# Moving SBUF tiles by 32, 64 or 96 bytes: spacers between the pools of a two-block transformer kernel

## The chip, the cores and the metric

The kernel runs on one core of one Trainium2 chip. The metric is the device time of one execution in microseconds (us), the median of several runs. TensorE is the engine PE of the profile (its weight loads are the row PEld), VectorE is DVE, ScalarE is ACT, GpSimd is POOL and SyncE is SP.

## The reference, cut to what matters

512 tokens of 1024 features pass two blocks. The first has two layers: a gated linear recurrence (HGRN2) and a differential attention, each followed by a squared-ReLU MLP of 4096 features. The second block has a state space branch and a windowed attention that are gated and summed, then a cross attention to 256 memory rows, then a third MLP of the same shape. All arithmetic is float32. Nearly all the work is products of activations with weights:

```python
def squared_relu_mlp(h, w_up, w_down):
    u = jax.nn.relu(h @ w_up)
    return (u * u) @ w_down
...
        proj = h @ w_in[i]
...
        merged = (jax.nn.sigmoid(gate_a) * (attn @ w_attn_branch[i])
                  + jax.nn.sigmoid(gate_b) * (ssd @ w_ssd_branch[i]))
        x = x + merged @ w_out[i]
        h = rmsnorm(x, norm_cross[i])
        x = x + cross_attention(h, rmsnorm(mem, norm_mem[i]), w_xq[i], w_xkv[i], w_xo[i])
        h = rmsnorm(x, norm_ffn[i])
        x = x + jnp.square(jax.nn.relu(h @ w_up[i])) @ w_down[i]
```

## The kernel before, in words

Every float32 product with weights is made of three products of the rounded type float32r. Each operand is held as a high part and a low part, and `mm3` (lines 397 to 400) sums high by high (L398), high by low (L399) and low by high (L400) into one PSUM tile:

```python
    def mm3(ps, a, b, first, last):
        nc.tensor.matmul(ps, a[0], b[0], start=first, stop=False)
        nc.tensor.matmul(ps, a[0], b[1], start=False, stop=False)
        nc.tensor.matmul(ps, a[1], b[0], start=False, stop=last)
```

The operand `a` is the stationary one: 128 columns of it are loaded into the array before each product. The operand `b` is the moving one: its 256 or 512 columns stream through the array. The profile names a product `out<-moving,stationary`.

The weights come from DRAM into the pool `raw` (three tiles of 4096 bytes per partition, names `raw`), and `Weights._split` (L115 to L127) splits each into a tile `hl` of the pool `spl` (six tiles of 8192 bytes: a high half and a low half). ScalarE writes the high part (L119, L125), VectorE, and in eight units GpSimd, the low part (L121, L126). The units are used in one fixed order. Loads run three tiles ahead and splits six tiles ahead of the first unit in use.

The activations lie in fixed tiles. `XTh` and `XTl` (pool `fix`) hold the transposed block input, `UAh` and `UAl` (pool `fix`) the first four tiles of 128 features of an intermediate result, and `UBh` and `UBl` (pool `bp`, opened much later) the other four. `h` and `ACC` (pool `fix`) hold the residual stream and a sum. The work tile `WK` (in the state space branch `WS`) and the evacuation tiles `y` hold what stays in float32, and `WR` the split keys of the attentions. `ident` (pool `const`) is the identity that every transpose streams.

Two kinds of loop call `mm3`:

- `feat` and `feat_first` put features on the partitions. They load 128 columns of `hl` as the stationary operand and stream the activations: 512 columns in `feat`, 256 in `feat_first` and for the memory rows (these lie in the `UB` tiles).
- `tok`, `tok2` and `last_rows` put tokens on the partitions. They load 128 tokens of `XT`, `UA` or `UB` as the stationary operand and stream `hl`: 256 columns in `tok`, 512 in `tok2` and `last_rows`.

The two calls, first of `feat`, then of `tok2`:

```python
                mm3(ps[:, :width], (wh[:, c], wl[:, c]), src(k), k == 0, k == n_k - 1)
...
                mm3(ps, (xh[:, tk], xl[:, tk]), w[k], k == 0, k == n_k - 1)
```

The order on each engine comes from a scheduler; the order of the weights from the list of units; the rest from waits on tiles.

The pools lie in SBUF one behind the other in the order in which they are opened: `const`, `fix`, `raw`, `spl`, `sm`, and then what the phases open (`bp`, `ev`, `wp` or `sp`). A tile begins at the next multiple of 32 bytes, so the lengths of the pools ahead of it set where it begins. All large tiles are multiples of 128 bytes long, so all tiles of one pool have the same remainder by 128.

Of the kernel before, what the change touches and what calls it, by code (L numbers as in the profile page):

```python
# [18 lines left out]
P = 128  # L19
# [7 lines left out]
def shape_constants():  # L27
    """Arrays that depend on shapes alone."""
    s = np.arange(P)[:, None]
    t = np.arange(P)[None, :]  # L30
    ident = np.eye(P, dtype=np.float32)
    lev = []
    for b in (1, 2, 4, 8, 16, 32, 64):
        same = (s // (2 * b)) == (t // (2 * b))
        lev.append(same & ((s // b) % 2 == 0) & ((t // b) % 2 == 1))
    lev.append(s <= t)
    masks = np.stack(lev, 1).astype(np.float32)
    d = np.arange(640) - 511
    n = np.abs(d)
    first = [8, 12, 16, 23, 32, 46, 64, 91]  # L40
    large = 8 + sum((n >= f).astype(np.int64) for f in first[1:])
    bucket = np.where(d > 0, 16, 0) + np.where(n < 8, n, large)
    onehot = -(bucket[None, :] == np.arange(32)[:, None]).astype(np.float32)
    rel = P + s - np.arange(3 * P)[None, :]
    band = np.where(np.abs(rel) <= 128, np.abs(rel), BIG).astype(np.float32)
    sel = np.zeros((P, 2, P), np.float32)
    sel[P - 1, 0, :] = 1.0
    sel[0, 1, :] = 1.0
    return {
        "c_ident": ident,  # L50
        "c_masks": np.ascontiguousarray(masks),
        "c_onehot": onehot,
        "c_band": band,
        "c_sel": sel,
    }


def vw(ap, off, dims):
    """A view of an SBUF/PSUM access pattern with its own free dimensions."""
    return bass.AP(tensor=ap.tensor, offset=ap.offset + off, ap=[list(ap.ap[0])] + [list(x) for x in dims])  # L60
# [6 lines left out]
class Weights:  # L67
    """Weight units in the order of their use: loaded ahead, split into two float32r parts ahead."""
# [13 lines left out]
    @staticmethod  # L82
    def _parts(sp):
        """a unit comes in parts of the tiles of rows that fill a place"""
        return max(1, sp[1] // Weights._rows(sp))
# [44 lines left out]
    def ahead(s, i):  # L130
        """i: the first unit that is still to be used."""
        n = s.first[-1]
        while s.n_spl < n and s.n_spl < s.first[i] + s.live:
            s._loads()
            s._split(s.n_spl)
            s.n_spl += 1
        s._loads()
# [10 lines left out]
    def get(s, name, hold=None):  # L148
        """The next unit; hold: the unit that stays the first one in use."""
        i = s.n_get  # L150
        assert s.specs[i][0] == name, (s.specs[i][0], name)
        s.n_get += 1
        s.ahead(i if hold is None else hold)
        assert len(s.hl[i]) == s._parts(s.specs[i]), name
        r = s.hl.pop(i)
        return [(h[:, k], l[:, k]) for h, l in r for k in range(h.shape[1])]


class Work:
    """Fixed places in one tile, by phase; what follows waits by the overlap of places."""  # L160
# [23 lines left out]
def together(*works, until=None):  # L184
    """the steps of several pieces of work in turn, up to the mark (if given) or the end of each"""
    works = list(works)
    while works:
        for w in list(works):
            try:
                mark = next(w)  # L190
            except StopIteration:
                works.remove(w)
                continue
            if until and mark == until:
                works.remove(w)


def body(ctx, tc, I, out, dbg=None, stop=None):
# [18 lines left out]
    # ------------------------------------------------------------ weights  # L217
# [93 lines left out]
    # split beside the norms at the ends of phases, where VectorE has the most to do  # L311
    WT.on_pool = {"m0up00", "m0up01", "m1up00", "m1up01", "sx0", "sbc0", "m2up00", "m2up01"}

    # ------------------------------------------------------------ fixed places
    h = fix.tile([P, NT, D], F32, name="h")
    ACC = fix.tile([P, NT * D], F32, name="ACC")
    acc = ACC.rearrange("p (t d) -> p t d", t=NT)
    XTh = fix.tile([P, 8, S], F32R, name="XTh")
    XTl = fix.tile([P, 8, S], F32R, name="XTl")
    UAh = fix.tile([P, 4, S], F32R, name="UAh")  # L320
    UAl = fix.tile([P, 4, S], F32R, name="UAl")

    ident = const.tile([P, P], F32, name="ident")
# [34 lines left out]
    # ------------------------------------------------------------ second arenas  # L358
# [12 lines left out]
    def open_wk(rounded=0):  # L371
        """the work tile, and places for operands of float32r products"""
        if "wctx" in st:
            st["wctx"].close()
        st["wctx"] = ExitStack()
        wp = st["wctx"].enter_context(tc.tile_pool(name="wp", bufs=1))
        n = 8424 - rounded
        st["wk"] = Work(wp.tile([P, n], F32, name="WK"), n)
        if rounded:
            r = wp.tile([P, rounded], F32R, name="WR")  # L380
            return [r[:, i:i + 512] for i in range(0, rounded, 512)]
# [20 lines left out]
    def split(dst, src, scale=None):  # L402
        """dst: float32r pair; src: PSUM or SBUF float32; scale: None or a per-partition factor."""
        hi, lo = dst
        if scale is None:
            nc.scalar.activation(out=hi, in_=src, func=AF.Copy)  # L406
            nc.vector.tensor_tensor(out=lo, in0=src, in1=hi.bitcast(F32), op=ALU.subtract)  # L407
        else:
            nc.scalar.activation(out=hi, in_=src, func=AF.Copy, scale=scale)  # L409
            nc.vector.scalar_tensor_tensor(out=lo, in0=src, scalar=scale, in1=hi.bitcast(F32), op0=ALU.mult, op1=ALU.subtract)  # L410

    def split_q(hd, ps):
        """two maps of 64 features, scaled: for each one tile with the high part where it is and the low part in the
        other half of the partitions"""
# [16 lines left out]
    def norm_places(first, n):  # L431
        """for the norms at the end of a phase: places from the end of the work tile"""
# [11 lines left out]
    def inv_sqrt(x, width):  # L444
        """x ** -0.5 without another table of ScalarE"""
# [11 lines left out]
    def row_rstd(src, k="", fine=False):  # L457
        """1 / rms of the rows; fine: the first half of a row alone as soon as it is there"""
# [10 lines left out]
    def gains(*aps):  # L469
        """norm weights on every partition, in the last places of the work tile"""  # L470
# [7 lines left out]
    def norm_T(t, src, gain, dst, fine=False):  # L478
        """rms norm of the rows of a token tile, and its transpose into the pair dst(kb) of [P, 4, n]"""
# [19 lines left out]
    # ------------------------------------------------------------ products  # L499
    def feat(w, src, evac, n_k=8, width=S):  # L500
        """features on partitions: two column tiles of the unit"""
# [8 lines left out]
    def feat_first(ws, src, evacs):  # L510
        """the same for the first units of a phase, half of the tokens at a time"""
# [14 lines left out]
    def tok(w, src, evac, n_k=8, tiles=NT):  # L526
        """tokens on partitions; evac(t, [P, 2, 256]) for two token tiles at a time"""
# [10 lines left out]
    def tok2(w, src, evac, n_k=8):  # L538
        """the same for units of 512 columns; evac(t, [P, 512])"""
# [8 lines left out]
    def last_rows(name, src, evac, done):  # L548
        """four resident units of the last part of a sum, one token tile after the other"""
# [21 lines left out]
    def post_norm(t, fine=False):  # L571
        """h += rms_norm(acc) * GP"""
# [11 lines left out]
    # ------------------------------------------------------------ MLP  # L584
# [35 lines left out]
    # ============================================================ layer 0: HGRN2  # L620
# [35 lines left out]
    def tables():  # L656
        # small tables
# [45 lines left out]
        # minus the relative bias, by distance  # L703
# [23 lines left out]
    def hgrn_head(hd, Z, G):  # L727
# [6 lines left out]
        def scores(b=0):  # L734
            """inside each chunk; for the larger blocks the pairs of blocks alone"""
# [136 lines left out]
    # ============================================================ MLP 0, and the norms of layer 1  # L872
# [10 lines left out]
    # ============================================================ layer 1: differential attention  # L883
# [7 lines left out]
    def diff_head(hd, k, v, place):  # L891
# [12 lines left out]
        def weights(i):  # L904
            """exponentials of row tile i for both maps"""
# [50 lines left out]
    def k_evac(j):  # L956
        """the high parts on both halves of the partitions, and the low parts"""
# [86 lines left out]
    # ============================================================ block 2: the state space branch  # L1044
    close_b()
    st["ctx"] = ExitStack()
    SW = 15592
# [74 lines left out]
    def bc64(ap):  # L1122
        """[P, 4] over 64 columns each"""
# [4 lines left out]
    class Group:  # L1128
        """four heads that share B and C"""
# [21 lines left out]
        def turn(s):  # L1151
            """x and B with the tokens on partitions"""
# [27 lines left out]
        def decays(s, c):  # L1180
            """the products of C and B inside a chunk with their decays and steps"""
# [10 lines left out]
        def first(s):  # L1192
            """products of C and B, decays, states"""
# [22 lines left out]
        def second(s):  # L1216
            """the chunks' results, gated"""
# [25 lines left out]
        def third(s):  # L1243
            """norm, features on partitions"""
# [51 lines left out]
    # ============================================================ block 2: windowed attention, gates  # L1296
# [4 lines left out]
    def gk_evac(n, ps):  # L1301
        """high and low parts, each on both halves of the partitions"""
# [12 lines left out]
    class Head:  # L1315
# [7 lines left out]
        def weights(s, n):  # L1323
            """exponentials of row tile n"""
# [87 lines left out]
    # memory for the cross attention  # L1412
# [25 lines left out]
    # ============================================================ block 2: cross attention  # L1438
# [71 lines left out]
    # ============================================================ block 2: MLP, last norm  # L1510
# [44 lines left out]
```

## Time and profile before

| | |
|---|---|
| time, median of 3 runs (lowest to highest) | 2630.79 us (2628.68 to 2632.54) |
| the profiled execution: time of the core, first to last instruction | 2630.0 us |
| mean granted TensorE clock | 0.992 of full speed |
| PE busy, PEld busy | 97%, 83% of the span |
| DVE, ACT, POOL busy | 56%, 43%, 7% of the span |
| DMA, mean over the span | 93 GB/s |

The span of the profiled execution is also its time: nothing lies around it. PE is called busy from a product's start to its modelled end, and consecutive products overlap in that reading: one of 512 columns is drawn 0.39 us long while the next begins 0.23 us later. So the busy time of PE and the mean duration of a product don't tell how fast products follow each other. That is read from the starts in the timeline, or from a stretch that holds nothing but products of one form: its length over their number.

### The profile page before, as it was taken

The numbers are of one execution on the slowest core, as the hardware profiler recorded it, in microseconds if no ns is written. First come the engines' busy times: TensorE is split into PE (matmuls) and PEld (weight loads), VectorE is DVE, ScalarE is ACT, GpSimd is POOL, SyncE is SP. The second block draws the span as 40 slices with busy tenths as digits, with TensorE's granted clock in tenths as the row PEclk, the third lists the DMA queues.
The fourth block names the chain that finished last, engine by engine and source line by source line (L and its number), as shares of the span: only waits on it lengthen the run. The fifth ranks groups of instructions, "written<-read, shape, count | busy, mean of one in ns | idle before, by whom it ended". The sixth has DMA issues, their size and how long they took to land.

```text
span 2630.0 us, 36139 instructions
## 1 busy us (share of the span) xinstructions
PE 2563.8 (97%) x14312; PEld 2196.0 (83%) x14312; DVE 1483.1 (56%) x2865; ACT 1137.8 (43%) x2153; POOL 183.5 (7%) x189
## 2 busy tenths in 40 slices
PE   8999999999999989999999999999999999999999
PEld 7899888888888878888887798888888789888887
DVE  5576453344666663333477888787554466534434
ACT  6333443233475553322365545553554436423322
POOL 1100210000201030000121000000000000100000
PEclk9999999999999999999999999999999999999999
DMA  5511233233233223333324334442211233233331
GB/s 178 137 52 62 81 104 94 91 96 101 85 91 94 73 81 97 96 96 96 92 77 129 97 97 115 105 110 80 81 41 49 87 98 121 80 91 97 101 97 56
DMA packets 198904, 243.65 MB, mean 93 GB/s; under 512 B 9744, under 2 KB 153344, under 8 KB 198736
## 3 DMA queue, kind: packets, MB, share of 16 engines
q1 hardware_dynamic: 188976, 207.97, 26.0%
q0 software_dynamic: 9040, 30.76, 4.6%
q10 hardware_dynamic: 720, 2.62, 0.3%
q8 instruction: 112, 1.84, 0.3%
q14 instruction: 56, 0.46, 0.1%
HBM read 239.05 MB, written 7.51 MB: 94 GB/s over the span
## 4 chain that ended last, share of the span: by engine, by line
PE 84%; DVE 5%; issue 4%; DMA 4%; ACT 3%; POOL 0%; SPq 0%; POOLq 0%; DVEq 0%; ACTq 0%
PE psm L398 23%; PE psm L399 23%; PE psm L400 23%; DMA WS<-aD 2%; PE pss L1356 2%; PE pss L740 1%; DMA raw<-in_a_w_in_dram 1%; PE pss L1331 1%; PE pss L398 1%; PE pss L400 1%; PE pss L399 1%; PE pss L912 1%; PE pss L1352 1%; DVE WS L1118 1%; DVE hl L121 1%
## 5 line engine op out<-in xcount | busy, mean ns | idle before, releaser
L398 PE MATMUL psm<-XTh,hl 128*128 128x512 f32 (+1 forms) x1400 | 533.9, 382 | 5.7 <-ACT XTh L406 3.0
L399 PE MATMUL psm<-XTl,hl 128*128 128x512 f32 (+1 forms) x1400 | 533.8, 381 | 4.7 <-DVE XTl L407 4.7
L400 PE MATMUL psm<-XTh,hl 128*128 128x512 f32 (+1 forms) x1400 | 532.6, 381 | 0.0
L119 ACT ACTIVATE hl<-raw 128x1024 fp32r<-128x1024 f32 x321 | 338.5, 1056 | 433.6 <-PE psm L400 373.2
L121 DVE TENSOR_TENSOR hl<-raw,hl 128x1024 fp32r<-128x1024 f32 x305 | 377.2, 1237 | 248.0 <-ACT hl L119 245.1
L398 PEld LDWEIGHTS psm<-XTh,hl 128*128 128x128 f32 x1400 | 264.6, 189 | 55.5 <-ACT XTh L406 4.1
L399 PEld LDWEIGHTS psm<-XTl,hl 128*128 128x128 f32 x1400 | 264.9, 189 | 53.0 <-DVE XTl L407 5.3
L400 PEld LDWEIGHTS psm<-XTh,hl 128*128 128x128 f32 x1400 | 264.8, 189 | 48.5 <-issue 0.4
L398 PE MATMUL psm<-hl,XTh 128*128 128x256 f32 (+1 forms) x928 | 285.7, 308 | 10.2 <-DVE sk L1207 2.8
L398 PE MATMUL psm<-hl,UAh 128*128 128x512 f32 (+1 forms) x768 | 276.7, 360 | 7.7 <-DVE ACC L566 5.9
L400 PE MATMUL psm<-hl,XTl 128*128 128x256 f32 (+1 forms) x928 | 283.7, 306 | 0.0
L399 PE MATMUL psm<-hl,XTh 128*128 128x256 f32 (+1 forms) x928 | 283.2, 305 | 0.2 <-DVE hl L126 0.2
L400 PE MATMUL psm<-hl,UAl 128*128 128x512 f32 (+1 forms) x768 | 274.3, 359 | 0.2 <-DVE UAl L410 0.2
L399 PE MATMUL psm<-hl,UAh 128*128 128x512 f32 (+1 forms) x768 | 274.2, 357 | 0.0
L398 PE MATMUL psm<-hl,UBh 128*128 128x512 f32 (+1 forms) x512 | 199.8, 390 | 1.1 <-ACT UBh L409 0.8
L399 PE MATMUL psm<-hl,UBh 128*128 128x512 f32 (+1 forms) x512 | 199.0, 389 | 0.0
L400 PE MATMUL psm<-hl,UBl 128*128 128x512 f32 (+1 forms) x512 | 198.9, 389 | 0.0
L398 PEld LDWEIGHTS psm<-hl,XTh 128*128 128x128 f32 x928 | 179.8, 194 | 19.2 <-ACT hl L119 3.2
L399 PEld LDWEIGHTS psm<-hl,XTh 128*128 128x128 f32 x928 | 179.8, 194 | 7.4 <-issue 1.1
L400 PEld LDWEIGHTS psm<-hl,XTl 128*128 128x128 f32 x928 | 179.6, 194 | 6.1 <-issue 0.5
L398 PEld LDWEIGHTS psm<-hl,UAh 128*128 128x128 f32 x768 | 146.6, 191 | 31.0 <-DVE ACC L566 6.8
L400 PEld LDWEIGHTS psm<-hl,UAl 128*128 128x128 f32 x768 | 146.5, 191 | 22.0 <-issue 0.9
(402 smaller groups left out, 3862.6 us busy)
## 6 DMA issues: line engine op xcount, KB each, us to landing
raw<-in_mlp_w_up_dram SPq DMA_DIRECT2D x64, 512.0 KB, 4.3
raw<-in_mlp_w_down_dram SPq DMA_DIRECT2D x64, 512.0 KB, 3.7
raw<-in_w_in_dram SPq DMA_DIRECT2D x60, 512.0 KB, 3.8
WS<-aD POOLq DMA_DIRECT2D x32, 512.0 KB, 6.5
raw<-in_w_up_dram SPq DMA_DIRECT2D x32, 512.0 KB, 4.0
raw<-in_w_down_dram SPq DMA_DIRECT2D x32, 512.0 KB, 3.7
raw<-in_w_in_dram SPq DMA_DIRECT2D x33, 256.0 KB, 3.9
raw<-in_a_w_in_dram SPq DMA_DIRECT2D x16, 512.0 KB, 3.8
```

The lines of the kernel that those rows point to most:

```text
L119: s.nc.scalar.activation(out=h, in_=r, func=AF.Copy)
L121: eng.tensor_tensor(out=l, in0=r, in1=h.bitcast(F32), op=ALU.subtract)
L398: nc.tensor.matmul(ps, a[0], b[0], start=first, stop=False)
L399: nc.tensor.matmul(ps, a[0], b[1], start=False, stop=False)
L400: nc.tensor.matmul(ps, a[1], b[0], start=False, stop=last)
L740: nc.tensor.matmul(ps[:, tk], H[:, tk], F[:, tk], start=True, stop=True)
L912: nc.tensor.matmul(pss[m][:, :N], q[r0], kl[r0, :N], start=False, stop=True)
L1118: nc.vector.scalar_tensor_tensor(out=dst[:, o0:o1], in0=ps[:, o0 + d:o1 + d], scalar=cw(j), in1=dst[:, o0:o1], op0=ALU.mult, op1=ALU.add)
L1331: nc.tensor.matmul(ps[:, :wd], uk(s.i)[s.p][:, n * P:(n + 1) * P], k_hl[x][s.kv][:, lo * P:hi * P], start=x == 0, stop=x == 1)
L1352: nc.tensor.transpose(pt[:, j * P:(j + 1) * P], e[:, j * P:(j + 1) * P], ident)
L1356: nc.tensor.matmul(po[r0, n * P:(n + 1) * P], v[:, lo + j, s.kv * 64:(s.kv + 1) * 64], PT[:, j * P:(j + 1) * P], start=j == 0, stop=j == h ...
```

## The change

Three small tiles are added that nothing reads, and three that hold work become shorter.

- `const` begins with a spacer `pad` of 32 bytes.
- In `fix`, a gap of 64 bytes stands between `ACC` and `XTh`, and another behind `UAl`.
- The work tiles `WK` (8424 words less those of `WR`) and `WS` (15592 words) are made 40 words shorter, which makes room for the spacers.

Each spacer is written once by a memset on POOL. No loop, operand, shape or wait is changed otherwise (the other lines of the diff take out comments and docstrings).

```diff
+    def gap(pool_, name):
+        nc.gpsimd.memset(pool_.tile([P, 16], F32, name=name), 0.0)
     h = fix.tile([P, NT, D], F32, name="h")
     ACC = fix.tile([P, NT * D], F32, name="ACC")
     acc = ACC.rearrange("p (t d) -> p t d", t=NT)
+    gap(fix, "gap0")
     XTh = fix.tile([P, 8, S], F32R, name="XTh")
     XTl = fix.tile([P, 8, S], F32R, name="XTl")
     UAh = fix.tile([P, 4, S], F32R, name="UAh")
     UAl = fix.tile([P, 4, S], F32R, name="UAl")
+    gap(fix, "gap1")
+    def spacer(pool_, words):
+        pad = pool_.tile([P, words], F32, tag="pad", name="pad", bufs=1)
+        nc.gpsimd.memset(pad, 0.0)
+    spacer(const, 8)
     ident = const.tile([P, P], F32, name="ident")
...
-        n = 8424 - rounded
+        n = 8384 - rounded
...
-    SW = 15592
+    SW = 15552
```

This is where the tiles begin in a partition of SBUF, as the remainder of the address by 128 bytes:

| tiles | before | with the change |
|---|---|---|
| `ident` | 0 | 32 |
| `h`, `ACC` | 96 | 0 |
| `XTh`, `XTl`, `UAh`, `UAl` | 96 | 64 |
| `raw`, `hl` | 96 | 0 |
| `UBh`, `UBl`, `GP`, `y`, `WK`, `WS` | 32 | 64 |
| `WR` | 64 | 64 |

Slices of the large operands start at multiples of 512 bytes inside their tiles, so this remainder is also that of every operand of `mm3`.

On PE, DVE, ACT and SP the instructions stand in the same order as before. POOL's queue has the three memsets more. Its beginning (the constants, a memset of the small tile `mhalf`, and the first loads of gains and tables into `ACC` and `band`) reads before:

```order
L1551 UNCONDITIONAL_BRANCH
L325 MEMSET mhalf 128x4
L345 DMA ACC<-in_a_norm_pre_dram 8x128
L659 DMA band<-in_c_band_dram 128x384
L672 DMA ACC<-in_conv_w_dram 96x128
```

The same place with the change, the spacers' tiles being `gap_80`, `gap_86` and `pad`:

```order
L1563 UNCONDITIONAL_BRANCH
L316 MEMSET gap_80 128x16
L316 MEMSET gap_86 128x16
L332 MEMSET pad 128x8
L337 MEMSET mhalf 128x4
L357 DMA ACC<-in_a_norm_pre_dram 8x128
L671 DMA band<-in_c_band_dram 128x384
```

The three memsets stand ahead of the first DMA of POOL's queue; nothing else has moved.

## Rows read from the trace of the kernel before

**Rows 1.** Profile page: span and the busiest engine.
```profile
span 2630.0 us, 36139 instructions
...
PE 2563.8 (97%) x14312; PEld 2196.0 (83%) x14312; DVE 1483.1 (56%) x2865; ACT 1137.8 (43%) x2153; POOL 183.5 (7%) x189
```

**Rows 2.** Profile page: chain of work that ended last, by engine.
```profile
PE 84%; DVE 5%; issue 4%; DMA 4%; ACT 3%; POOL 0%; SPq 0%; POOLq 0%; DVEq 0%; ACTq 0%
```

**Rows 3.** Lines by form, PE, first line of `mm3`: count | busy us, mean ns | idle.
```profile
L398 PE MATMUL psm<-XTh,hl 128*128 128x512 f32 x1232 | 484.1, 393 | 2.6 <-DVE WS L1118 2.4 <-DVE ss L451 0.3
...
L398 PE MATMUL psm<-hl,XTh 128*128 128x256 f32 x800 | 235.1, 294 | 9.4 <-DVE sk L1207 2.8 <-ACT XTh L406 2.5 <-DVE WS L1118 2.3
...
L398 PE MATMUL psm<-hl,UAh 128*128 128x512 f32 x512 | 201.2, 393 | 1.4 <-ACT UAh L409 0.8 <-DVE ACC L566 0.3 <-DVE h L566 0.3
...
L398 PE MATMUL psm<-hl,UBh 128*128 128x512 f32 x480 | 190.3, 396 | 1.1 <-ACT UBh L409 0.8 <-DVE ACC L566 0.3
...
L398 PE MATMUL psm<-hl,UAh 128*128 128x256 f32 x256 | 75.5, 295 | 6.2 <-DVE ACC L566 5.6 <-ACT ACC L564 0.7
...
L398 PE MATMUL psm<-hl,XTh 128*128 128x512 f32 x128 | 50.6, 396 | 0.8 <-ACT WK L1388 0.8
...
L398 PE MATMUL psm<-XTh,hl 128*128 128x256 f32 x160 | 46.6, 295 | 3.0 <-ACT XTh L406 3.0
L398 PE MATMUL pss<-XTh,hl 128*128 128x256 f32 x160 | 46.2, 289 | 0.0
...
L398 PE MATMUL psm<-hl,UBh 128*128 128x256 f32 x32 | 9.5, 295 | 0.0
...
L398 PE MATMUL psm<-UBh,hl 128*128 128x256 f32 x32 | 9.0, 280 | 0.0
```

**Rows 4.** Windows of products alone: stretch, length, busy (x) by engine, PEclk, DMA.
```profile
2535.72:2579.26 43.54, 43.54 (x193) 36.05 (x192) 20.90 (x24) 16.42 (x22) 0.00 (x0) 1.00 0.38 119
2579.26:2601.02 21.76, 21.76 (x97) 18.02 (x96) 9.53 (x12) 4.19 (x5) 0.00 (x0) 1.00 0.08 25
2601.02:2623.19 22.17, 22.17 (x96) 17.86 (x95) 9.99 (x17) 5.02 (x11) 0.57 (x1) 1.00 0.18 67
1850.69:1862.20 11.51, 11.51 (x98) 11.51 (x96) 5.34 (x8) 5.56 (x8) 0.00 (x0) 1.00 0.32 91
```

**Rows 5.** Timeline of PE, first and last of two series of 256 columns.
```profile
2185.95 0.28 PE L398 MATMUL psm<-UBh,hl 128*128 128x256 f32 x1
...
2193.61 0.28 PE L400 MATMUL psm<-UBh,hl 128*128 128x256 f32 x1
...
2194.72 0.28 PE L399 MATMUL psm<-hl,UBh 128*128 128x256 f32 x1
...
2199.95 0.28 PE L400 MATMUL psm<-hl,UBl 128*128 128x256 f32 x1
```

**Rows 6.** Windows of float32 work on PE: transposes, products of 256 and of 128 columns.
```profile
1769.00:1770.20 1.20, 1.20 (x14) 1.20 (x12) 0.56 (x1) 1.18 (x4) 0.45 (x1) 1.00 0.50 176
1630.92:1632.43 1.51, 1.51 (x8) 1.33 (x7) 1.41 (x5) 0.63 (x1) 0.00 (x0) 1.00 0.33 115
...
1793.60:1794.49 0.89, 0.89 (x11) 0.89 (x9) 0.89 (x2) 0.89 (x2) 0.00 (x0) 1.00 0.02 5
```

**Rows 7.** Windows, PE instructions that read `hl` alone: state space branch, first stretch.
```profile
1315.00:1841.00 526.00, 416.73 (x2393) 0.98 0.38 101
0.00:131.50 131.50, 91.85 (x529) 0.99 0.55 158
```

**Rows 8.** Chain that ended last in these two stretches, by line.
```profile
by line: issue 18.3%; DMA WS<-aD 11.9%; PE psm L398 11.1%; PE psm L400 10.8%; PE psm L399 10.7%; DVE WS L1118 3.8%; PE pss L1238 3.3%; DVE hl L121 2.6%; ACT WS L1189 1.9%; PE pss L1169 1.6%; PE pss L1225 1.6%; PE pss L1227 1.5%; ACT hl L119
...
by line: DMA raw<-in_a_w_in_dram 22.3%; PE psm L398 17.7%; PE psm L400 17.4%; PE psm L399 17.3%; PE pss L740 5.8%; PE pss L795 3.4%; PE pss L491 2.3%; DVE hl L126 2.2%; ACT hl L125 1.7%; PE pss L744 1.5%; DVE WK L758 1.0%; PE pss L711 0.9%;
```

**Rows 9.** Timeline of POOL at the start: two memsets in a row.
```profile
0.30 0.11 POOL L1543 MEMSET const-bfloat16-1.0<- 128x1 bf16 x1
0.33 0.11 POOL L1543 MEMSET const-uint8-127<- 128x1 uint8 x1
```

## The prediction

> **What bounds the kernel now.** The first view is the page's table of engines: PE is busy for 2563.8 of 2630.0 us, DVE, the next, for 56% [rows 1]. The second is the chain of work that ended last: 84% of it is PE [rows 2]. So nearly everything that makes products follow each other faster or slower reaches the end. How fast they follow is read from stretches that hold nothing but products of one form (length over number), and there the granted clock is 1.00, that is 2.4 GHz: 512 columns are 213.3 ns, 256 are 106.7 ns.
>
> The reader is to see that these products are never that fast, and that their spacing goes with the place of the operands:
> - 512 columns of `XT` over stationary `hl`: 43.54 us for 192, 226.8 ns each. 512 columns of `hl` over stationary `UA`: 21.76 us for 96, 226.7 ns [rows 4].
> - the same product a moment later, 512 columns of `hl` over stationary `UB`: 22.17 us for 95, 233.4 ns [rows 4].
> - 256 columns of `hl` over `XT`: 11.51 us for 96, 119.9 ns [rows 4].
> - 256 columns of `hl` over `UB`: from 2194.72 to 2199.95 us 46 products, 113.7 ns. 256 columns of `UB` over `hl`: from 2185.95 to 2193.61 us 65 products, 117.8 ns [rows 5].
>
> `XT`, `UA` and `hl` all begin at remainder 96; `UB` alone begins at 32, so 64 bytes away from `hl`. Above the bare columns the five forms lose 13.4, 20.0, 13.2, 7.0 and 11.1 ns. In columns of 0.417 ns these are 32, 48, 32, 17 and 27. With four-byte columns 16 columns are 64 bytes: four of the five losses lie near a multiple of that, one to three pieces of 64 bytes. That no wait is involved is seen in the windows: PE is busy throughout. As a measure of what remains without such a loss I take the float32 work: 11 transposes of 128 columns start in 1.20 us, 109.1 ns each, and 7 passes of 256 columns in 1.51 us, 215.7 ns each [rows 6]. They go at half the pace and lose 2.4 ns above their columns.
>
> **The change, part by part.** *The operands of the products.* Before, every one begins in the middle of a piece of 64 bytes (remainders 96 and 32); afterwards none does, and the operand that is loaded lies 64 bytes from the one that streams (0 and 64). No row shows a float32r product with both operands on multiples of 64 bytes, so its spacing is bounded. Below: bare columns, 213.3 and 106.7 ns, a gain of 13.4 or more. Above: what the rows with 64 bytes between the operands show, 233.4 ns for 512 columns, a loss of 6.6, and 117.8 or 113.7 ns for 256. I take columns plus 2.4 ns, 215.7 and 109.1: the whole pieces of 64 bytes look like an extra fetch for a first half piece and collisions of two streams that walk over the same memory, and the change takes the ground from both. This is a reading of five numbers, not shown.
>
> The numbers of products are three times those of L398, since `mm3` has three of each [rows 3]:
> - 512 columns, `XT` and `UA`: 3 x (1232 + 512 + 128) = 5616, by 226.8 - 215.7 = 11.1 ns: 62.3 us.
> - 512 columns, `UB`: 3 x 480 = 1440, by 17.7 ns: 25.5 us.
> - 256 columns, `XT` and `UA`: 3 x (800 + 256 + 160 + 160) = 4128, by 119.9 - 109.1 = 10.8 ns: 44.6 us.
> - 256 columns, `UB`: 96 by 4.6 and 96 by 8.7 ns: 1.3 us.
>
> That is 133.7 us. Not all of it reaches the end. In the state space branch (1315 to 1841 us) 2393 of these products run [rows 7], at 11 ns 26.3 us; the chain there is products of `mm3` for 11.1 + 10.8 + 10.7 = 32.6%, the rest is the load of `aD`, issue, DVE and ACT [rows 8]. I keep a third and give back 17.7 us: what is late next there is the broadcast load of `aD` and the DVE work behind it. In the first 131.5 us 529 products [rows 7] would save 5.8 us; 52% of the chain is theirs, and the load of `in_a_w_in` holds 22% [rows 8]: 2.8 us go back. Sum: 133.7 - 20.5 = 113.2 us, 85% of the gross gain.
>
> *Other operands.* `ident` leaves remainder 0 for 32, while `WK`, `WS` and `y` go from 32 to 64. A transpose that streams `ident` from 0 takes 109.1 ns; a float32 product with both operands at 32 takes 0.89 us for 8, 111.3 ns [rows 6]. So some 800 transposes may lose 2.2 ns each (1.8 us) and as many or more float32 products gain it. I set the two against each other: 0, within 3 us either way. For DVE, ACT and DMA no row of this kernel ties a duration to a remainder; most of their work is beside PE's [rows 1], and I cost it at nothing. If that cover went, the splits of `hl` would be late first.
>
> *The memsets.* Two small memsets in a row on POOL start 0.03 us apart [rows 9]; three put the first load of POOL's queue back by 0.1 us, at most 0.33 us if their 0.11 us add up. Behind it waits the first split of weights. Below what is told apart here.
>
> The profiled execution took 2630.0 us, 0.8 us under the median of the runs. 2630.0 - 113.2 = 2516.8; I predict 2517 us.
>
> A rule of the Trainium skill speaks against all of this: the page "SBUF — State Buffer", section "A bandwidth-pool intuition that's wrong (but worth ruling out)", gives TensorE a second, independent read port for weight loads, and its section "SBUF: two separate sides" says that PE never waits on anyone there. By it, no placing of the operands could matter, and the sum would be 0 instead of 113 us (rival D). The trace doesn't agree: 226.7 and 233.4 ns for the same form, 44 us apart in one loop [rows 4].
>
> **The rivals.**
> - *B, half of it.* Only the half piece at the start goes, 16 columns or 6.7 ns in each of the 11280 products: 75.2 us, and 63.9 at 85%. 2566 us. For it: 256 columns of `hl` over `UB` lose 17 columns, the least of all, with nothing but the start to blame. Against: it needs a collision that is the same 64 bytes apart as at no distance.
> - *E, only products of 256 columns gain.* The 512 ones keep 226.8 ns (those of `UB` come down to it): 1440 x 6.6 = 9.5 us, with 45.9 us of the 256 ones 55.4, at 85% 47. 2583 us. For it: 64 bytes apart helped 256 columns and not 512.
> - *C, slower.* 64 bytes between the operands are what costs: 512 columns of `XT` and `UA` take the 233.4 ns of `UB`. 5616 x 6.6 = 37.1 us are lost. 256 columns gain what `UB`'s rows show: 3168 with `hl` streaming by 6.2 ns, 960 with `XT` streaming by 2.1 ns, 21.7 us. The net loss is 15.4 us: 2645 us. For it: the only rows of 512 columns with that distance. Against: in them both operands also begin in the middle of a piece. It decides from about 230.6 ns for 512 columns upward, where 5616 x 3.8 ns eat the 21.7 us.
> - *D, no change.* The remainder doesn't matter, and `UB` is slower or faster for another reason. 2630 us. Against: rows 4 and 5 differ by form and place alone.
>
> **How the numbers follow.** The forecast has a chance of 0.46, B 0.17, E 0.13, something between the forecast and B 0.04, C 0.14, D 0.06. The lowest time is that of bare columns: 2.4 ns less in 11280 products, 27 us, 23 at 85%: 2494, and with 3 us for the other operands about 2490. Up to E with its own spread the range is 2490 to 2600 us and holds 0.80. The forecast's own range is 2490 to 2545. About 0.2% (5 us) is what a measurement of this kernel can tell from no change. Faster by more: forecast, B, E and what lies between, 0.80, less 0.01 for spread: 0.79. Within it: D and the edges of the others, 0.07. Slower: C, 0.14.
>
> **What would show each step right or wrong.** In stretches of one form the profile of the changed kernel should show about 216 ns for 512 columns, alike for `XT`, `UA` and `UB`, and about 109 ns for 256. 220 and 113 would be B, 227 and 109 E, 233 C. The state space branch should shorten by less than its products do, with DVE's share up. The forecast would be wrong if 512 columns stay above 220 ns, if the two directions (activations or weights streaming) part, if the splits of `hl` no longer keep ahead of PE in the MLPs, or if the granted clock falls with denser work.

## The result, and the profile with the change

| | before | with the change |
|---|---|---|
| time, median of 4 runs each (lowest to highest) | 2631.66 us (2628.68 to 2635.60) | 2645.98 us (2645.73 to 2646.09) |
| the profiled execution, first to last instruction | 2630.0 us | 2644.0 us |

The kernel became slower: ratio 1.0059, 95% interval 1.0043 to 1.0074, some 14 us. The forecast of 2517 us and its range are missed, on the wrong side; rival C had 2645 us.

The page of the changed kernel, its span and the table of engines:

```profile
span 2644.0 us, 36142 instructions
...
PE 2579.8 (98%) x14312; PEld 2187.7 (83%) x14312; DVE 1481.9 (56%) x2865; ACT 1137.2 (43%) x2153; POOL 185.1 (7%) x192
```

Against [rows 1] PE alone has become busier by more than 2 us: 16.0 us more for the same 14312 products (the weight loads, PEld, have 8.3 us less). The three more instructions on POOL are the memsets. PE's share of the chain is 84% as in [rows 2]. So nothing points to a new wait; the products themselves follow each other more slowly. That is read where [rows 4] and [rows 5] read it, in stretches of one form. The windows of the changed kernel (stretch, length, PE busy and products, granted clock, DMA share, GB/s; the x counts also a product or two that began ahead of the window, so lengths are divided by 192, 96, 95, 96, 96 and 48):

```profile
2547.84:2592.63 44.79, 44.79 (x194) 1.00 0.35 116
2592.63:2615.03 22.40, 22.40 (x97) 1.00 0.08 25
2615.03:2637.19 22.16, 22.16 (x96) 1.00 0.18 66
2094.49:2116.47 21.98, 21.98 (x97) 1.00 0.46 142
1858.50:1869.81 11.31, 11.31 (x97) 1.00 0.33 93
726.33:731.77 5.44, 5.44 (x50) 1.00 0.00 2
```

- 512 columns of `XT` over `hl` take 233.3 ns, of `hl` over `UA` 233.3, of `hl` over `UB` 233.3 (lines 1 to 3). Before, the first two took 226.8 and 226.7, `UB` 233.4 [rows 4]. `XT` and `UA` have come up to `UB`; `UB` has not come down.
- The fourth line is `hl` over `UA` again, in another stage: 229.0 ns. Two spacings now occur for one form.
- 256 columns of `hl` over `XT` take 117.8 ns, of `XT` over `hl` 113.3 (lines 5 and 6), against 119.9 for the former in [rows 4].

Where the 14.0 us of span arose is seen when the program is cut at the same products in both traces. Four of the seven stretches, first of the kernel before: the MLP behind the recurrence, the MLP behind the differential attention, most of the state space branch, the last MLP.

```profile
366.83:693.14 326.31, 326.31 (x1433) 1.00 0.31 96
...
998.83:1325.59 326.76, 326.76 (x1435) 1.00 0.30 94
1325.59:1782.00 456.41, 428.26 (x2705) 0.98 0.40 107
...
2293.80:2623.19 329.39, 329.39 (x1441) 1.00 0.29 90
```

The same four with the change:

```profile
366.09:697.75 331.66, 331.66 (x1432) 1.00 0.30 95
...
1002.02:1334.15 332.13, 332.13 (x1434) 1.00 0.29 93
1334.15:1789.81 455.66, 428.05 (x2705) 0.98 0.39 106
...
2302.42:2637.19 334.77, 334.77 (x1441) 1.00 0.28 89
```

Each MLP takes 5.35, 5.37 and 5.38 us more, 16.1 together; everything else gives 2.1 back, 0.75 of it in the long third stretch. PE is busy from end to end of an MLP, so nothing there can hide a slower product. In the last MLP's stretch, summed from start to next start, 672 products with `XT` streaming cost 4.3 us more, 384 over `UA` 1.1, and 383 over `UB` 0.1 less.

The same sum over the whole kernel, before to after, idle time between starts included: 512 columns over or of `XT` and `UA` +24.5 us, 512 columns over `UB` -0.3, 256 columns over or of `XT` and `UA` -8.1, all the rest -1.9; together 14.2, the way from the first product to the last.

### The profile page after: what moved, and what is told of

Its sections match the earlier page's. It is cut to its first block, busy times and chain, and to the rows that moved or that the text cites. A ratio compares the mean times of both kernels' runs of the same rounds, so it can differ in the third digit from the quotient of the medians.

```text
span 2644.0 us, 36142 instructions
## 1 busy us (share of the span) xinstructions
PE 2579.8 (98%) x14312; PEld 2187.7 (83%) x14312; DVE 1481.9 (56%) x2865; ACT 1137.2 (43%) x2153; POOL 185.1 (7%) x192
## 4 chain that ended last, share of the span: by engine, by line
PE 84%; DVE 5%; issue 4%; DMA 4%; ACT 3%; POOL 0%; SPq 0%; POOLq 0%; ACTq 0%; DVEq 0%
PE psm L410 23%; PE psm L411 23%; PE psm L412 23%; DMA WS<-aD 2%; PE pss L1368 2%; PE pss L752 1%; DMA raw<-in_a_w_in_dram 1%; PE pss L1343 1%; PE pss L924 1%; PE pss L411 1%; PE pss L410 1%; PE pss L412 1%; PE pss L1364 1%; PE pss L945 1%; DVE hl L121 1%
## 5 line engine op out<-in xcount | busy, mean ns | idle before, releaser
L410 PE MATMUL psm<-XTh,hl 128*128 128x512 f32 (+1 forms) x1400 | 539.9, 386 | 5.5 <-ACT XTh L418 3.0
L411 PE MATMUL psm<-XTl,hl 128*128 128x512 f32 (+1 forms) x1400 | 539.6, 386 | 4.7 <-DVE XTl L419 4.7
L412 PE MATMUL psm<-XTh,hl 128*128 128x512 f32 (+1 forms) x1400 | 538.3, 385 | 0.0
```

## The experiments

Eleven kernels ran. By the main theory the distance between the stationary and the moving operand counts (rival C's ground). Against it stood that the place of an operand within a piece of 64 bytes counts, and that something else which the spacers bring does. Each timed kernel is compared with the kernel before, run beside it on the same chip (there 2632.8 to 2634.4 us, as a median). Where a spacer needs room, `WK` or `WS` give up about as much; the code cuts leave these lines out. In experiment 1 the distance is counted from the moving operand to the stationary one, from experiment 5 on from the activations to the weights in `hl`, whichever of the two is loaded; both modulo 256 bytes unless a longer one is named.

**1. A table of distances, by itself.** A small kernel that leaves the whole computation out: series of 40 products, the stationary operand put 0 to 248 bytes behind a multiple of 256 from the moving one, in steps of 8.

> This kernel leaves the whole computation out: PE alone runs 64 series of 40 float32r products, 32 with 512 moving columns and then 32 with 256, the moving operand always at remainder 0 by 128 bytes, the stationary one 0, 8, 16, ... 248 bytes further. Theory 1 (the distance of the two operands by 128 bytes sets the spacing): 512 columns at about 226.7 ns at distance 0 and 128, at 229 to 233 ns at 64 and 192; 256 columns at about 120 ns at 0 and 128, at 113 to 118 ns at 64; the two halves of each table alike. Theory 2 (the place inside a piece of 64 bytes sets it, as the prediction had it): 216 to 220 ns and 109 to 113 ns wherever the distance is a multiple of 64, more elsewhere. Theory 3 (neither; other work in the kernel slows the products): the same spacing at every distance.

Measured: 512 columns took 228.3 to 234.4 ns at nearly all distances, 226.6 at 120, 232.4 at 128 and 233.4 at 64 bytes. 256 columns took 119.9 at 0, 117.8 at 64, 118.6 at 128, 117.8 at 192 and 113.3 at 88. The place of the stationary operand alone moves the spacing, but 128 bytes do not repeat 0. The series at 0 bytes for 512 columns, the first of the kernel, began at half the pace (products 427 ns apart), so it is no measure.

**2. The alignment without the distance.** The spacer of 32 bytes in `const` alone, added to the kernel before: `XT`, `UA` and `hl` at remainder 0, still at distance 0.

```diff
+    gap(const, "pad", 8)
```

> The kernel before with the spacer of 32 bytes in the first pool alone: operands of float32r products on multiples of 64 bytes as after the change, but XT, UA and hl at distance 0 and UB at 64, as before it. Theory 1 (distance): no change, 2631 us within 5 us; 512 columns of XT at 226.7 ns, 256 columns at 120 ns. Theory 2 (pieces of 64 bytes): faster, 6.7 ns in each of 11280 products, about 2566 us. Theory 3 (the identity's place, or that of the float32 tiles, costs the time): slower, towards 2646 us.

Measured: 2633.54 against 2634.27 us, ratio 0.9992 (0.9979 to 1.0005). The windows of the last MLP with `XT` streaming (192) and over `UB` (95):

```profile
2531.46:2575.01 43.55, 43.55 (x193) 1.00 0.38 120
2596.77:2618.94 22.17, 22.17 (x96) 1.00 0.18 67
```

226.8 and 233.4 ns, as in [rows 4]. Moving the operands together from the middle of a piece of 64 bytes to its start changes nothing.

**3. The distance without the alignment.** The two gaps of 64 bytes alone (`XT` and `UA` at remainder 32, `hl` at 96; `WK` and `WS` 24 words shorter).

```diff
+    gap(fix, "gap0", 16)
...
+    gap(fix, "gap1", 16)
```

> The kernel before with the two gaps of 64 bytes around XT and UA alone: hl stays at 96, XT, UA and UB lie at 32, so the distance is 64 everywhere while every operand still begins in the middle of a piece of 64 bytes and the identity stays at 0. Theory 1 (distance): as the changed kernel, 2646 us within 5 us; 512 columns of XT at about 233 ns. Theory 2 (pieces): the products as before the change, about 2631 us. Theory 3 (identity and float32 tiles): about 2631 us.

Measured: 2647.68 us, ratio 1.0052 (1.0035 to 1.0068): the whole loss. The window with `XT` streaming (192):

```profile
2544.25:2589.04 44.79, 44.79 (x193) 1.00 0.36 116
```

233.3 ns. The gap behind `UAl` puts `hl` 64 bytes further from `XT` and `UA`, and that is the cost.

**4. `UB` moved by 64 bytes.** `UB` then lies at `hl`'s own remainder by 128.

```diff
+        gap(bp, "gapb", 16)
```

> The kernel before with a gap of 64 bytes ahead of UB alone: XT, UA, UB and hl all at remainder 96, distance 0 everywhere. Theory 1 (distance): the 1440 products of 512 columns that read UB go from 233.4 to 226.7 ns, 9.6 us less, and 192 of 256 columns from 114 to 118 ns to 120 ns, 0.8 us more: about 2622 us. Theory 2 and theory 3: no change, 2631 us within 5 us.

Measured: 2635.82 us, ratio 1.0003 (0.9991 to 1.0015). The window over `UB` with 512 columns (51):

```profile
955.99:967.89 11.90, 11.90 (x52) 1.00 0.01 2
```

Still 233.3 ns. An expectation by a period of 128 bytes is missed: `UB`, 51520 bytes behind `hl` and so 64 past a multiple of 256, now lies 128 past one.

**5. The table with the kernel's own loops.** Again a small kernel without the computation: series of 96 products in the order of `feat`, `tok` and `tok2`, distances up to 512 bytes, all of it twice.

> This kernel leaves the whole computation out: PE alone runs the product loops with their own order of operands and slices (feat with 512 columns, tok with 256, tok2 with 512; 96 products a series) at distances of 0 to 512 bytes between the tiles in steps of 32, each series twice. Theory 1a (the spacing goes with the distance by 512 bytes): 226.7 ns for 512 columns and 120 ns for 256 at 0 and 512, 228 to 234 and 113 to 118 ns at every other one. Theory 1b (by 256 bytes): the low values for 512 columns at 256 too. Theory 1c (by 128 bytes, and run 4 failed for another reason): at 128, 256 and 384 too. Theory 4 (the spacing depends on how a series begins, not on the distance): the two takes of a series differ as much as the distances do.

Measured: the two takes agree. Nine of the series with activations streaming, 512 columns, at distances 0, 32, 64, 96, then 192, 224, 256, 320 and 448 bytes:

```profile
35.98:57.75 21.77, 21.77 (x97) 1.00 0.00 0
57.75:80.14 22.39, 22.39 (x97) 1.00 0.00 1
80.14:102.54 22.40, 22.40 (x97) 1.00 0.00 1
102.54:125.02 22.48, 22.48 (x97) 1.00 0.00 1
...
169.73:191.72 21.99, 21.99 (x98) 1.00 0.00 1
191.72:214.11 22.39, 22.39 (x97) 1.00 0.00 1
214.11:235.87 21.76, 21.76 (x97) 1.00 0.00 0
235.87:258.27 22.40, 22.40 (x98) 1.00 0.00 1
...
280.58:302.56 21.98, 21.98 (x98) 1.00 0.00 1
```

A series of 96 takes 226.8 ns a product at 0, 233.2 to 234.2 at 32, 64 and 96, 229.1 at 192, and 226.7 at 256 again; 320 repeats 64, 448 repeats 192. For 256 columns of weights the distances 0, 64, 192 and 256 bytes:

```profile
324.33:335.84 11.51, 11.51 (x97) 1.00 0.01 1
...
347.16:358.47 11.31, 11.31 (x99) 1.00 0.01 1
...
392.63:403.54 10.91, 10.91 (x98) 1.00 0.01 2
...
414.90:426.41 11.51, 11.51 (x98) 1.00 0.01 1
```

119.9, 117.8, 113.6 and 119.9 ns. For 512 columns of weights the distances 64 and 192 bytes:

```profile
515.69:537.68 21.99, 21.99 (x98) 1.00 0.00 0
604.97:627.36 22.39, 22.39 (x97) 1.00 0.00 0
```

229.1 and 233.2 ns, the other way round than with activations streaming. There the weights are loaded, here the activations: counted from the moving operand to the stationary one, 64 here is 192 there. By that count the two forms of 512 columns agree within 0.2 ns at every distance up to 256 bytes except 128 (232.4 and 233.4).

The period is 256 bytes, and distance 0 is the best place of this table for 512 columns (by steps of 8 bytes, experiment 1 has another as good, 120) and the worst shown here for 256. DMA is idle and no other engine touches the operands in these series, so the spacing needs no neighbour.

**6 and 7. `UB` at a multiple of 256 bytes from `hl`.** The kernel before with 192 bytes ahead of `UB` (distance 512 by the larger period), and with 448 (distance 256 modulo 512).

```diff
+        gap(bp, "gapb", 48)
```

> The kernel before with 192 bytes ahead of UB, which puts UB at a whole multiple of 512 bytes from hl, as XT and UA are (before, 320 bytes beyond one). Theories 1a and 1b: 512 columns over UB at 226.7 ns in place of 233.4, 1440 x 6.7 = 9.6 us less, 0.8 us more for 256 columns: about 2622 us, ratio 0.9966. Theory 1c: no better than the run with 64 bytes, 2634 us. Theory 4: no change.

> The kernel before with 448 bytes ahead of UB, which puts UB 256 bytes beyond a multiple of 512 from hl. Theory 1b: as the run with 192 bytes, about 2622 us. Theory 1a: 512 columns over UB stay near 233 ns, 2631 us within 5 us. Theory 4: no change.

Measured: 2625.52 us, ratio 0.9962 (0.9948 to 0.9977), and 2624.95 us, ratio 0.9961 (0.9948 to 0.9974). The window over `UB` (95 products), of the first, then of the second:

```profile
2596.45:2617.99 21.54, 21.54 (x97) 1.00 0.18 66
```

```profile
2595.27:2616.80 21.53, 21.53 (x96) 1.00 0.18 66
```

226.7 and 226.6 ns, where [rows 4] has 233.4. Both multiples serve alike; the period is 256, and the 512-column products over `UB` are 8.4 us shorter in sum. The gain in time is 7.3 and 7.8 us by the medians, 10 us by the ratios.

**8. The change with gaps of 256 bytes.** The changed kernel with both gaps four times as long: the spacers, the memsets and `ident`'s new place remain, `WK` and `WS` are 88 words shorter still, the distance is 0 again.

```diff
-        nc.gpsimd.memset(pool_.tile([P, 16], F32, name=name), 0.0)
+        nc.gpsimd.memset(pool_.tile([P, 64], F32, name=name), 0.0)
```

> The changed kernel with gaps of 256 bytes in place of 64 (the work tiles 88 words shorter again): hl lies a whole multiple of 256 bytes from XT and UA, as before the change, everything else as after it. Theory 1b (distance by 256 bytes): 512 columns of XT and UA at 226.7 ns, 256 columns at 120 ns, time as before the change, about 2632 us, ratio 0.999 to 1.002. If spacers, shorter work tiles or the identity's place cost anything: between that and 2646 us.

Measured: 2631.80 us, ratio 0.9989 (0.9978 to 0.9999), so the loss is gone. The window with `XT` streaming (192):

```profile
2534.68:2578.23 43.55, 43.55 (x193) 1.00 0.37 119
```

226.8 ns. Spacers, memsets, shorter work tiles and the place of `ident` cost nothing that can be told apart.

**9. The other side.** The changed kernel with 192 bytes in the second gap: the same remainders by 128, distance 192 in place of 64, where the table has 229 and 113.4 ns.

```diff
-        nc.gpsimd.memset(pool_.tile([P, 16], F32, name=name), 0.0)
+        nc.gpsimd.memset(pool_.tile([P, 48 if name == "gap1" else 16], F32, name=name), 0.0)
```

> The changed kernel with a second gap of 192 bytes in place of 64: every remainder by 128 bytes is as after the change, but hl now lies 192 bytes beyond a multiple of 256 from XT and UA, not 64. Theory 1b with the table of run 5: 512 columns of XT over hl 228.9 ns (3696 x 2.1 = 7.8 us more than before), of hl over XT and UA 233.3 (1920 x 6.6 = 12.7 us more), 256 columns of hl 113.4 ns (3168 x 6.5 = 20.6 us less), of XT 117.8 (960 x 2.1 = 2.0 us less): net 2 us less than before, about 2630 us, no change that can be told. A theory of the distance by 128 bytes: as the changed kernel, 2646 us.

Measured: 2641.94 us, ratio 1.0022 (1.0012 to 1.0032). Missed. Windows with `XT` streaming, 192 products each, and with 256 columns of `hl` over `XT` (96):

```profile
2455.17:2499.13 43.96, 43.96 (x193) 1.00 0.38 118
2543.93:2588.73 44.80, 44.80 (x194) 1.00 0.37 116
1854.52:1865.42 10.90, 10.90 (x97) 1.00 0.36 96
```

229.0 ns in one stretch and 233.3 in the same loop 45 us later; 256 columns 113.5 here, 117.8 in other stretches. At this distance there are two rhythms, and the table shows only the one that its series fell into.

**10. Each form where the table has it best.** The kernel before with `UB` at distance 0 and each weight unit shifted inside a larger place: 192 bytes where weights stream in 256 columns, 64 where activations stream in 256, none where a product has 512. For room `sm` gets four buffers instead of six, and `WK` and `WS` become shorter.

```diff
-        hl = s.spl_p.tile([P, 2, kp * w], F32R, tag="hl", name="hl")
+        o = s.shift(name)
+        hl = s.spl_p.tile([P, 2112], F32R, tag="hl", name="hl")[:, o:o + 2 * kp * w].rearrange("p (a n) -> p a n", a=2)
...
-    sm = pool("sm", 6)
+    sm = pool("sm", 4)
...
+        nc.gpsimd.memset(bp.tile([P, 16], F32, name="gapb"), 0.0)
```

> The kernel before, with each unit of weights put where the table of run 5 is lowest for the loop that reads it: UB at a whole multiple of 256 bytes from hl; units that tok streams 192 bytes further inside their place, units of feat_first 64 bytes, the others 0 (places of hl 8448 bytes; to make room the small pool keeps 4 tiles of a name in place of 6, and the work tile is 232 words shorter). Theory 1b: 512 columns 226.7 ns everywhere (9.6 us less), 256 columns of hl 113.4 ns (3264 x 6.5 = 21 us less, of which some 6 us are lost in the state space branch), 256 columns of activations 113 to 118 ns (2 to 6 us less): about 2602 us, ratio 0.987 to 0.992. If fewer small tiles cost waits, less of it.

Measured: 2612.33 us, ratio 0.9914 (0.9901 to 0.9928), faster than both kernels: 22 us gained, where the expectation has some 29 (the ratio lies at the weak end of the expected range). Windows: `XT` streaming (192), `hl` over `UB` (95), and two of 256 columns (95 each):

```profile
2515.32:2558.84 43.52, 43.52 (x194) 1.00 0.38 120
2580.60:2602.13 21.53, 21.53 (x96) 1.00 0.18 66
1645.91:1656.69 10.78, 10.78 (x96) 1.00 0.32 90
1767.51:1778.70 11.19, 11.19 (x98) 1.00 0.37 110
```

226.7 and 226.6 ns for 512 columns; 113.5 and 117.8 for 256, again two rhythms.

**11. What picks the rhythm.** A small kernel without the computation.

> The whole computation is left out; only series of 96 products are run, each once behind each of six things: 96 products with the operands at distance 0 (512 columns with activations streaming, 256 columns, 512 columns with weights streaming), four float32 products of 128 columns, four products of 64 columns, and one product with VectorE adding on 1024 columns meanwhile. Distances: 192 and 64 bytes for activations streaming (512 columns) and for weights streaming (256 columns), 64 bytes for 512 columns of weights. Theory P (the place alone sets the spacing, and the loops of the full kernel differ from the measured series by something else): behind all six the spacing is that of the table, 228.9 and 233.3 ns for the 512 columns of activations, 113.4 and 117.8 ns for 256, 228.9 ns for 512 columns of weights. Theory M (two steady rhythms exist at a distance other than 0, and what ran ahead picks one): the same series takes 228.9 ns behind some of the six and 233.3 ns behind others, or 113.4 and 117.8 ns.

Measured: theory M holds. The windows of five of the thirty series, 95 products each: 512 columns of activations at 192 bytes, behind 96 products of the same form at distance 0, then behind one product with VectorE adding; 256 columns of weights at 192 bytes, behind 256 columns of weights, then behind 512 columns of activations; 256 columns of weights at 64 bytes.

```profile
58.61:80.36 21.75, 21.75 (x97) 1.00 0.00 1
203.38:225.54 22.16, 22.16 (x96) 1.00 0.00 1
461.43:472.21 10.78, 10.78 (x97) 1.00 0.00 0
438.61:449.80 11.19, 11.19 (x97) 1.00 0.01 2
585.13:596.32 11.19, 11.19 (x97) 1.00 0.01 1
```

They take 228.9, 233.3, 113.5, 117.8 and 117.8 ns. For 512 columns at 192 bytes five of the six things ahead lead to 228.9 and one to 233.3; 512 columns of weights at 64 bytes do the same. 256 columns of weights at 192 bytes take 113.4 behind two and 117.8 behind four. At 64 bytes activations always take 233.4 and 256 columns of weights always 117.8, whatever runs ahead. Counted again from the moving operand to the stationary one, the five kinds of series stand at two distances only: at 64 bytes 512 columns have one rhythm (233.4) and 256 columns two, at 192 bytes 512 columns have two and 256 columns one (117.8). The changed kernel fits: `XT` streaming in 512 columns (64) has no stretch at 229.0, `hl` over `UA` (192) has both, and 256 columns of `hl` (192) take 117.8 but for a few short stretches at 113.3. A rhythm, once taken, holds to the end of its series. Whether the VectorE work or the single product ahead of it made the difference was not told apart.

## Why the prediction was wrong, step by step

- *PE bounds the kernel, and the spacing of products is what the change moves.* Right. 14.2 us of products make 14.0 us of span.
- *The spacing goes with the place of the operands.* Right, and by the right rows: in [rows 4] `UB` was the odd one. The fault lies in what was read from it.
- ***512 columns, XT and UA: 5616 by 11.1 ns.*** This is the step that failed. The value of 215.7 ns came from float32 work, which has another pace, and from the thought that the change takes away half pieces of 64 bytes and collisions. Experiment 2 takes away the half pieces: 226.8 ns remain. The change did not take away a distance, it brought one: between `XTh` and the first `hl` lay `XT`, `UA` and `raw`, 49152 + 12288 = 61440 bytes, from `UAh` on 16384 + 12288 = 28672, both whole multiples of 256, and 64 bytes were put between. The spacing became 233.3 ns, in part 229.0, in place of 215.7, and the term measured +24.5 us in place of -62.3.
- *512 columns, UB: 1440 by 17.7 ns.* Wrong for the same reason: `UB` stayed at its distance, and gained 0.3 us of 25.5. Experiments 6 and 7 show what it could have: 226.7 ns, by a place at a multiple of 256.
- *256 columns: 4128 by 10.8 ns.* The sign was right, the size not: 8.1 us of 44.6. They took 113.3 to 117.8 ns, not 109.1.
- *The share that gives itself back, 20.5 us.* Never tried, since there was no net gain to give back. The state space stretch became 0.75 us shorter, with no sign of a wait that grew.
- *Other operands and the memsets at nothing.* Right (experiment 8).
- *Rival C.* Its sum of 2645 us stood 1 us from the median, and its 233.4, 117.8 and 113.7 ns all occur; that the sum came so near is partly luck. Both its terms were too large: 24.5 us lost for 37.1, 8.1 gained for 21.7. C left out which of the two operands lies ahead. In `UB`'s rows `UB` lies 64 bytes past a multiple of 256 from `hl`; with the change `hl` lies 64 past one from `XT` and `UA`. So nearly all products of 256 columns of `hl` over `XT` took 117.8 ns, not C's 113.7; of `XT` over `hl` 113.3 in part, not 117.8; and 512 columns of `hl` over `UA` 229.0 in part, not 233.4. What spoke against C, that both operands also begin in the middle of a piece, is what experiment 2 shows to count for nothing. C should have had the larger chance: it alone took its prices from rows with 64 bytes between the operands.
- *Rival D, and the rule of the Trainium skill beside it* (page "SBUF — State Buffer", section "A bandwidth-pool intuition that's wrong (but worth ruling out)": a second, independent read port for weight loads). The measurements decide against D once more: with DMA idle and only ScalarE's copies out of PSUM beside PE, experiment 5 moves the same product from 226.7 to 234.2 ns by the distance alone. Whether it is at these ports that the operands disturb each other, no run shows.
- *Slips of the working that change nothing.* The two stretches called 44 us apart begin 22 us apart [rows 4]. The products of rival B are 11376, not 11280 (both forms of 96 with `UB` count), which moves its time by under 1 us.

What stays open: why distance 0 serves 512 columns and is worst for 256, why the direction counts, and how what runs ahead sets the rhythm. That the loading of one operand meets the stream of the other in the same memory is argued, not shown.

## What to carry to other kernels

Before tiles are moved, work out for each product the distance from its moving to its stationary operand modulo 256 bytes, before and after, and look in the trace for a row with just that distance, in that direction: it is the price, not an ideal spacing that no row shows. In this kernel 512 columns wanted distance 0 and 256 columns a distance that breaks it, and a spacer ahead of `UB`, the one tile that was off, is worth 7 to 10 us where the change as made cost 14. Equal remainders by 128 are not enough (experiment 4); a period has to be measured before it is used.

## What the runs showed of the hardware that was not expected

- The spacing of float32r products, each with its own weight load, depends on the distance from the moving to the stationary operand with a period of 256 bytes: in the kernel's own loops, by steps of 32 bytes and past the first products of a series, 512 columns take 226.7 ns at 0 and 228.9 to 234.3 elsewhere, 256 columns 120.0 at 0 and 113.3 to 119.9 elsewhere (experiment 5), at a granted clock of 1.00 throughout.
- At some distances two steady rhythms exist (228.9 and 233.3 ns for 512 columns at 192 bytes; 113.4 and 117.8 ns for 256 columns at 64 bytes, both counted from the moving to the stationary operand), and what ran ahead of a series decides which (experiment 11); at distance 0 every stretch that was read had one.
